# Embedding gate and final norm of a hybrid decoder step on 384 and 192 tokens instead of 288 and 288

## The chip, the cores and the metric

One of the cores of a Trainium2 chip runs the whole program: one inference step of a one-layer decoder for 576 tokens, 512 of a prompt and 64 of samples. The metric is the device time of one execution in microseconds (us). The engines are TensorE (PE, its weight loads shown as PEld), VectorE (DVE), ScalarE (ACT), GpSimd (POOL) and SyncE (SP), whose queue issues the transfers.

## The reference, cut to what matters

The change touches the end of the step: the gate by the per-layer embedding, and the final norm.

```python
gate = jax.nn.sigmoid(rmsnorm(x, lp['ple_norm_g']) @ lp['ple_gate_w'])
x = x + gate * (pe.astype(x.dtype) @ lp['ple_proj'])
...
y_prompt = rmsnorm(y_p, final_norm_g)
y_sample = rmsnorm(y_s, final_norm_g)
```

Here rmsnorm(x, g) is x times the inverse root of the mean square over the 1024 channels, times g. Everything is float32.

## The kernel before, in words

Activations lie transposed: eight tiles x1[0] to x1[7] (named res in the profile) hold 128 channels each on the partitions, with all T = 576 tokens along the row. A matrix product of 1024 by 1024 is therefore 8 output tiles m times 8 input tiles k. To keep float32 accuracy at the faster data type float32r, each weight and each activation is split into a high and a low part (wh, wl; xb0h, xb0l and so on), and each product is three matmuls: high by high, high weight by low activation, low weight by high activation. An output tile of some tokens takes 24 matmuls that add into one bank of PSUM.

The 576 tokens are worked in two halves of HF = 288. For the end of the step:

- `norm_half` makes the ple norm of one half for all eight tiles: DVE scales (L268, xnf), ACT rounds to the high part (L269, xb*k*h), DVE or POOL subtracts for the low part (L270, xb*k*l; POOL for odd k). Both halves are issued ahead of the next step.
- ple_proj is multiplied for all tokens; ACT copies it to the tiles pps (pp, L1383).
- The eight gate weights are loaded and split ahead of use (tiles wg, acth/actl, wh/wl), then the four heads' mLSTM matrices kv are loaded (L1395) into the same ring of nine acth/actl buffers, so that all but the first wait for gate matmuls.
- For each half, for each m: 24 matmuls (`dense_half`, L193); ACT takes tanh of half of it (gth, L1402); DVE multiplies by pps (L1403) and adds into x1[m] (L1404); ACT squares (L253) and DVE adds the square to acc (L254); the last m is squared on DVE (L251).
- Then `rms_half`: three matmuls with acc as weights and a column of ones sum over the channels (L234); DVE scales and adds EPS (L235, rsc); POOL raises to the power -0.5 (L216); ACT spreads the columns (L238, rsb); PE transposes back to rows (L241). DVE multiplies the eight tiles by that and by the gain (yo, L1410), and SP sends them out in five transfers (L1411).
- At the very end the state's matrices, four matmuls a head (L1416), a copy (co, L1418) and a transfer (L1419).

PSUM gives the gates three banks in turn. Tile pools give buffers by tag; a tile that takes a buffer again waits for the last use of it. The tag "u" with two buffers holds gth and co, "y" two, "ac" two, "ws" three. The order on each engine is set by a scheduler from the program and its own estimates; each engine's queue then runs strictly in that order, so what is listed first also waits first.

Of the kernel before, what the change touches and what calls it, by code (L numbers as in the profile page):

```python
# [7 lines left out]
F32 = mybir.dt.float32  # L8
F32R = mybir.dt.float32r
AF = mybir.ActivationFunctionType  # L10
ALU = mybir.AluOpType
# [4 lines left out]
P = 128  # L16
D = 1024
# [4 lines left out]
HF = T // 2  # L22
KD = D // P
NFF = 22
RT = 14
EPS = 1e-6
# [69 lines left out]
def build(tc, nc, I, O):  # L96
    from contextlib import ExitStack

    V, S, G, TE, SY = nc.vector, nc.scalar, nc.gpsimd, nc.tensor, nc.sync
# [9 lines left out]
    with st0:  # L109
# [8 lines left out]
        def bank(tag="m", name="pm"):  # L118
            if tag == "d" and turn:
                tag = turn[0]  # L120
                turn.append(turn.pop(0))
            return ps.tile([P, 512], F32, tag=tag, name=name, bufs=nbufs[tag])
# [5 lines left out]
        def vcol(name, k=0, rows=P):  # L128
            return vec[0:rows, VEC[name] + k:VEC[name] + k + 1]
# [6 lines left out]
        ones = cc("ones")  # L136
# [47 lines left out]
        def dense_half(pm, ws, xs, hf, ks=None):  # L184
            c = slice(hf * HF, (hf + 1) * HF)
            n = len(xs)
            for k in ks or range(n):
                half_k(pm, ws, xs[k], k, n, c)
# [25 lines left out]
        def inv_sqrt(t, n):  # L214

            G.tensor_tensor(t, t, nhalf[0:t.shape[0], :].to_broadcast([t.shape[0], n]), ALU.pow)  # L216
# [10 lines left out]
        HB = (0, P, HF - P)  # L227

        def rms_half(pl, acc, hf, pt="m"):

            pm = bank(pt)
            cols = pl.tile([P, 3], F32, tag="rsc", name="rsc", bufs=2)
            for w, o in enumerate(HB):
                TE.matmul(pm[:, w:w + 1], acc[:, hf * HF + o:hf * HF + o + P], ones[:, 0:1], start=True, stop=True)  # L234
            V.tensor_scalar(cols, pm[:, 0:3], 1.0 / D, EPS, ALU.mult, ALU.add)  # L235
            inv_sqrt(cols, 3)
            bc = pl.tile([P, 3, P], F32, tag="rsb", name="rsb", bufs=2)
            S.copy(bc, cols.unsqueeze(2).to_broadcast([P, 3, P]))  # L238
            b = bank(pt)
            for w, o in enumerate(HB):  # L240
                TE.transpose(b[:, o:o + P], bc[:, w, :], ident)  # L241
            return b[:, 0:HF]

        def add_squares(pl, acc, x, k, hf, eng=None, on_v=False):
            c = slice(hf * HF, (hf + 1) * HF)
            if k == 0:
                (eng or V).tensor_tensor(acc[:, c], x[:, c], x[:, c], ALU.mult)
            else:
                sq = pl.tile([P, HF], F32, tag="sq", name="sq", bufs=3)
                if on_v:  # L250
                    V.tensor_tensor(sq, x[:, c], x[:, c], ALU.mult)  # L251
                else:
                    S.activation(sq, x[:, c], AF.Square)  # L253
                (eng or V).tensor_tensor(acc[:, c], acc[:, c], sq, ALU.add)  # L254
# [121 lines left out]
        with ExitStack() as stn:  # L376
            npool = pool(stn, "n1")
            acc = npool.tile([P, T], F32, name="acc")
# [13 lines left out]
            pm = bank("m")  # L392
# [60 lines left out]
            for hf in range(2):  # L453
                if hf:
                    norm_half(npool, xt, rsr[:, half(1)], 1, "norm1_g", xs1)
                for k in range(KD):
                    for i in range(2):
                        TE.matmul(lps["if"][hf][:, 0:HF], w2[k // 4][:, k % 4, :], xs1[k][i][:, half(hf)],
                                  start=k == 0 and i == 0, stop=k == KD - 1 and i == 1)
# [762 lines left out]
        rpool = pool(stF, "res")  # L1222
        x1 = [rpool.tile([P, T], F32, name=f"res{m}") for m in range(8)]
        acc = rpool.tile([P, T], F32, tag="acc", name="acc")
# [39 lines left out]
        xs2 = new_split(pool(stS, "xn2", side="right"), "xb")  # L1264
# [3 lines left out]
        with ExitStack() as stw:  # L1268
# [5 lines left out]
            for hf in range(2):  # L1274
                c = slice(hf * HF, (hf + 1) * HF)
                for m in range(8):
                    pm = bank("d", "pd")
# [15 lines left out]
        fp = pool(stf_, "ffn")  # L1293
# [63 lines left out]
        for g, (j0, nj) in enumerate(GR):  # L1357
            acts = [up(j0 + j) for j in range(nj)]
            if g == 2:
                SY.dma_start(O["o_fconv"], o_f)  # L1360
                pes = []
                for k in range(2):
                    pt = fp.tile([P, T], F32, tag="ac", name="pe", bufs=2)
                    SY.dma_start(pt, I["pe"][k])
                    pes.append(split(fp, "act", pt, bufs=ACT))
            for m in range(8):
                pss = dense(I["f_down"][m, :, j0:j0 + nj, :], acts)
                for hf in range(2):
                    c = slice(hf * HF, (hf + 1) * HF)
# [14 lines left out]
        wg = []  # L1384
# [7 lines left out]
        for h in range(4):  # L1392
            kv.append([fp.tile([P, 4, n], F32, tag=t, name="kv", bufs=ACT) for t, n in (("acth", P), ("actl", 129))])
            for t, c in zip(kv[h], (slice(0, 512), slice(512, 1028))):
                SY.dma_start(t, d_kv[h][:, c].rearrange("p (w x) -> p w x", w=4))  # L1395
        for hf in range(2):
            c = slice(hf * HF, (hf + 1) * HF)
            for m in range(8):
                pm = bank("d", "pd")
                dense_half(pm, wg[m], xs2, hf)  # L1400
                th = fp.tile([P, HF], F32, tag="u", name="gth", bufs=2)
                S.activation(th, pm[:, 0:HF], AF.Tanh, scale=0.5)  # L1402
                V.scalar_tensor_tensor(th, th, 1.0, pps[m][:, c], ALU.add, ALU.mult)  # L1403
                V.scalar_tensor_tensor(x1[m][:, c], th, 0.5, x1[m][:, c], ALU.mult, ALU.add)  # L1404
                add_squares(rpool, acc, x1[m], m, hf, on_v=m == KD - 1)
            rs = rms_half(rpool, acc, hf, "mr"[hf])
            for k0, n, t, b in ((0, 2, "y", 2), (2, 2, "ac", 2), (4, 2, "y", 2), (6, 1, "ac", 2), (7, 1, "ws", 3)):
                yo = fp.tile([P, n, HF], F32, tag=t, name="yo", bufs=b)
                for k in range(k0, k0 + n):
                    V.scalar_tensor_tensor(yo[:, k - k0, :], x1[k][:, c], vcol("final_norm_g", k), rs, ALU.mult, ALU.mult)  # L1410
                SY.dma_start(O["o_y"][k0:k0 + n, :, c].rearrange("k p t -> p k t"), yo[:, 0:n, :])  # L1411

        for h in range(4):
            pc = bank("scsr"[h])
# [105 lines left out]
```

## Time and profile before

| | us |
|---|---|
| median of three runs | 1073.62 |
| the three runs | 1073.53, 1073.62, 1078.61 |
| the profiled execution | 1070.66 |
| its span | 1068.8 |
| first gate matmul, from the span's start | 1002.58 |
| last gate matmul starts | 1055.31 |
| final scalings of the second half start | 1061.28 |

The profile is one execution with times from the start of its span; the span is 1.86 us shorter than the execution's own time. The granted TensorE clock was 0.996 of full over the span. The chain of waits is read backwards from the last instruction: at each step it names what released the work that ended last. In the timelines a row has start, length, engine, line, operation, output and inputs, and in brackets the idle time before it with what ended that.

### The profile page before, as it was taken

What the parts mean: (1) busy time and instruction counts of PE and PEld (TensorE: products, weight loads), DVE (VectorE), ACT (ScalarE), POOL (GpSimd) and SP (SyncE); (2) the same over time, 40 slices, a digit from 0 to 9 for tenths busy, and PEclk for the clock granted to TensorE, in tenths of its full rate; (3) what the DMA queues carried; (4) which work ended last, traced back from release to release, by engine and by line L of the source; (5) the groups of instructions that cost most, each with busy time, mean ns of one, the idle gap of its engine ahead of it and who ended that gap; (6) DMA issues with size and microseconds to landing.
All of it is one profiled execution on the core that took longest, in us unless ns stands there. A gap on an engine that the chain in (4) does not pass through costs nothing.

```text
span 1068.8 us, 23108 instructions
## 1 busy us (share of the span) xinstructions
PE 1045.1 (98%) x8991; PEld 1009.0 (94%) x8991; DVE 777.0 (73%) x1645; ACT 508.8 (48%) x1072; POOL 254.5 (24%) x394
## 2 busy tenths in 40 slices
PE   8899999999999999999999999999999999999996
PEld 7899999999989988999999999999999999999996
DVE  7887657876786676356775799945998569975864
ACT  7684634462553344334343465522565236553822
POOL 7622112221131021001401253200343005410300
PEclk9999999999999999999999999999999999999999
DMA  7243412442342322446850312322233322342513
GB/s 252 95 127 93 108 53 58 103 141 60 88 143 75 81 84 91 143 151 234 263 181 1 116 37 93 110 90 75 85 99 97 102 70 90 94 117 67 165 40 123
DMA packets 90894, 114.74 MB, mean 107 GB/s; under 512 B 35617, under 2 KB 45217, under 8 KB 90785
## 3 DMA queue, kind: packets, MB, share of 16 engines
q1 hardware_dynamic: 90784, 113.27, 34.7%
q8 instruction: 70, 1.15, 0.4%
q14 instruction: 40, 0.32, 0.1%
HBM read 94.79 MB, written 18.45 MB: 106 GB/s over the span
## 4 chain that ended last, share of the span: by engine, by line
PE 90%; DVE 4%; DMA 4%; ACT 1%; issue 1%; SPq 0%; POOLq 0%; DVEq 0%; ACTq 0%
PE pd L193 55%; PE pd L306 20%; PE pm L655 1%; PE pm L1106 1%; PE pm L1136 1%; PE pm L835 1%; PE pm L809 1%; DMA yin<-d_y 1%; PE pm L910 1%; DVE xnf L268 1%; PE pm L917 1%; PE pm L1199 1%; PE pm L775 0%; DMA d_y<-og 0%; DMA wr<-i_w_out 0%
## 5 line engine op out<-in xcount | busy, mean ns | idle before, releaser
L169 ACT CAST wh<-wr 128x512 fp32r<-128x512 f32 (+2 forms) x170 | 101.7, 599 | 173.4 <-PE pd L193 140.7
L170 DVE TENSOR_TENSOR wl<-wr,wh 128x512 fp32r<-128x512 f32 (+2 forms) x170 | 118.8, 702 | 82.4 <-ACT wh L169 80.8
L193 PE MATMUL pd<-actl,wh 128*128 128x288 f32 x384 | 111.9, 295 | 0.0
L193 PE MATMUL pd<-acth,wl 128*128 128x288 f32 x384 | 111.4, 295 | 0.0
L193 PE MATMUL pd<-acth,wh 128*128 128x288 f32 x384 | 110.3, 295 | 0.0
L193 PEld LDWEIGHTS pd<-actl,wh 128*128 128x128 f32 x384 | 71.8, 188 | 0.0
L193 PEld LDWEIGHTS pd<-acth,wl 128*128 128x128 f32 x384 | 71.6, 188 | 0.0
L193 PEld LDWEIGHTS pd<-acth,wh 128*128 128x128 f32 x384 | 71.1, 188 | 0.1
L294 ACT CAST wh<-ws 128x512 fp32r<-128x512 f32 x76 | 47.1, 619 | 48.9 <-PE pd L306 24.8
L295 DVE TENSOR_TENSOR wl<-ws,wh 128x512 fp32r<-128x512 f32 x76 | 58.1, 765 | 8.4 <-ACT wh L294 7.9
L300 POOL TENSOR_TENSOR ws<-wr 128x512 f32<-128x512 f32 x19 | 31.7, 1670 | 96.9 <-DVE wl L295 54.1
L294 ACT CAST wh<-wr 128x512 fp32r<-128x512 f32 x57 | 35.3, 619 | 38.5 <-PE pd L306 24.0
L1333 POOL COPY o_f<-u 128x2 f32<-128x2 f32 x22 | 26.6, 1209 | 110.8 <-DVE u L1330 109.2
L295 DVE TENSOR_TENSOR wl<-wr,wh 128x512 fp32r<-128x512 f32 x57 | 39.5, 693 | 7.3 <-ACT wh L294 7.2
L216 POOL TENSOR_TENSOR rsc<-rsc,nhalf 128x3 f32<-128x3 f32 x8 | 9.3, 1167 | 131.1 <-DVE rsc L235 131.1
L1342 DVE SCALAR_TENSOR_TENSOR y<-u,vec,y 128x592 f32<-128x592 f32 x44 | 38.5, 875 | 1.2 <-ACT y L1340 1.0
L253 ACT ACTIVATE sq<-res 128x288 f32<-128x288 f32 x40 | 17.7, 445 | 36.0 <-DVE res L1279 18.5
L193 PE MATMUL pd<-mgh,ol 128*128 128x288 f32 x112 | 33.0, 296 | 0.0
L193 PE MATMUL pd<-mgl,oh 128*128 128x288 f32 x112 | 33.0, 295 | 0.0
L193 PE MATMUL pd<-mgh,oh 128*128 128x288 f32 x112 | 32.8, 295 | 0.0
L1370 DVE TENSOR_TENSOR res<-res,pd 128x288 f32<-128x288 f32 x48 | 20.9, 450 | 15.7 <-PE pd L193 15.5
L193 PE MATMUL pd<-xa0h,wh 128*128 128x288 f32 x86 | 26.4, 307 | 3.0 <-ACT zr L352 1.6
(825 smaller groups left out, 3949.4 us busy)
## 6 DMA issues: line engine op xcount, KB each, us to landing
wr<-i_w_in SPq DMA_DIRECT2D x92, 256.0 KB
wr<-i_f_up SPq DMA_DIRECT2D x88, 256.0 KB
wr<-i_f_down SPq DMA_DIRECT2D x32, 256.0 KB
d_th<-gst SPq DMA_DIRECT2D x16, 288.0 KB
th<-d_th SPq DMA_DIRECT2D x16, 288.0 KB
wr<-i_w_br SPq DMA_DIRECT2D x16, 256.0 KB
wr<-i_w_out SPq DMA_DIRECT2D x16, 256.0 KB
wr<-i_ple_gate SPq DMA_DIRECT2D x16, 256.0 KB
```

What stands on the lines that cost most here:

```text
L169: S.copy(wh[:, 0:nk, :], wr[:, 0:nk, :])
L170: V.tensor_tensor(wl[:, 0:nk, :], wr[:, 0:nk, :], wh[:, 0:nk, :], ALU.subtract)
L193: TE.matmul(pm[:, 0:HF], w[:, k % 4, :], a[:, c], start=k == 0 and i == 0, stop=k == n - 1 and i == 2)
L253: S.activation(sq, x[:, c], AF.Square)
L268: V.scalar_tensor_tensor(xn, xt[k][:, c], vcol(gname, k), rs, ALU.mult, ALU.mult)
L294: S.copy(wh, w)
L295: V.tensor_tensor(wl, w, wh, ALU.subtract)
L300: e.tensor_tensor(t, a, b, ALU.add)
L306: TE.matmul(pm[:, 0:HF], w[a][:, k, :], xs[k][b], start=not more and k == 0 and i == 0, stop=k == 3 and i == 2, skip_group_check=more)
L1333: G.tensor_copy(o_f[:, j, 0:2], u[:, TP:TP + 2])
L1342: V.scalar_tensor_tensor(y, u[:, i:i + 592], w(i), y, ALU.mult, ALU.add)
L1370: V.tensor_tensor(x1[m][:, c], x1[m][:, c], pss[hf][:, 0:HF], ALU.add)
```

## The change

The gate and the final norm run on a first group of 384 tokens and a second of 192. The matmuls are written out in the loop (L1409 of the changed program). `rms_half` becomes a call of `rms_part`, which takes several operands for the column sums and any blocks of columns (three of 128 for 384 tokens; two of 128 that overlap for 192). The square of the last tile (sqw) is no longer added into acc, but is a second operand of the column sums. The square of the first tile goes straight from ACT into acc. The first group's outputs are eight single tiles from "y" and "ws"; the second's are three pairs on DVE and one pair, for the first two tiles, that POOL multiplies by a copy of the norm's rows and ACT scales by the gain.

```diff
+        def rms_part(pl, accs, c0, width, blocks, pt):
...
-            for w, o in enumerate(HB):
-                TE.matmul(pm[:, w:w + 1], acc[:, hf * HF + o:hf * HF + o + P], ones[:, 0:1], start=True, stop=True)
+            for w, o in enumerate(blocks):
+                for i, (a, z) in enumerate(zip(accs, (c0, 0))):
+                    TE.matmul(pm[:, w:w + 1], a[:, z + o:z + o + P], ones[:, 0:1], start=i == 0, stop=i == len(accs) - 1)
...
-        for hf in range(2):
-            c = slice(hf * HF, (hf + 1) * HF)
+        for g, (c0, w, blocks) in enumerate(((0, 384, (0, P, 2 * P)), (384, 192, (0, 64)))):
+            c = slice(c0, c0 + w)
             for m in range(8):
-                pm = bank("d", "pd")
-                dense_half(pm, wg[m], xs2, hf)
-                th = fp.tile([P, HF], F32, tag="u", name="gth", bufs=2)
-                S.activation(th, pm[:, 0:HF], AF.Tanh, scale=0.5)
+                pm = bank("d", "pd")[:, 0:w]
+                for k in range(KD):
+                    wh, wl = wg[m][k // 4]
+                    for i, (a, b) in enumerate(((wh, 0), (wh, 1), (wl, 0))):
+                        TE.matmul(pm, a[:, k % 4, :], xs2[k][b][:, c], start=k == 0 and i == 0, stop=k == KD - 1 and i == 2)
+                th = fp.tile([P, 384], F32, tag="u", name="gth", bufs=2)[:, 0:w]
+                S.activation(th, pm, AF.Tanh, scale=0.5)
...
-                add_squares(rpool, acc, x1[m], m, hf, on_v=m == KD - 1)
-            rs = rms_half(rpool, acc, hf, "mr"[hf])
-            for k0, n, t, b in ((0, 2, "y", 2), (2, 2, "ac", 2), (4, 2, "y", 2), (6, 1, "ac", 2), (7, 1, "ws", 3)):
+                if m == 0:
+                    S.activation(acc[:, c], x1[m][:, c], AF.Square)
+                else:
+                    sq = fp.tile([P, 384], F32, tag="ac", name="sqw", bufs=2)[:, 0:w]
+                    if m < KD - 1:
+                        S.activation(sq, x1[m][:, c], AF.Square)
+                        V.tensor_tensor(acc[:, c], acc[:, c], sq, ALU.add)
+                    else:
+                        V.tensor_tensor(sq, x1[m][:, c], x1[m][:, c], ALU.mult)
+            rs = rms_part(rpool, (acc, sq), c0, w, blocks, "mr"[g])
+            n0 = 0
+            if g:
...
+                rsc = fp.tile([P, 192], F32, tag="u", name="rsc2", bufs=2)
+                S.copy(rsc, rs)
+                yo = fp.tile([P, 2, 192], F32, tag="ac", name="yo2", bufs=2)
+                for k in range(2):
+                    G.tensor_tensor(yo[:, k], x1[k][:, c], rsc, ALU.mult)
+                    S.activation(yo[:, k], yo[:, k], AF.Copy, scale=vcol("final_norm_g", k))
+                SY.dma_start(O["o_y"][0:2, :, c].rearrange("k p t -> p k t"), yo)
+                n0 = 2
+            step = 1 + g
+            for i, k0 in enumerate(range(n0, KD, step)):
+                t, nb = ("ws", 3) if i % 2 and not g else ("y", 2)
+                yo = fp.tile([P, step, w], F32, tag=t, name="yo", bufs=nb)
```

On PE, where the gates begin, stood the following before. The outputs pd_13497, pd_13527 and pd_13559 are the gates of tiles m = 0, 1 and 2 in the three banks; xb0h and xb0l are the two parts of the norm's tile k = 0; the last name is the weight.

```order
L193 MATMUL pd_13497<-xb0h_7372,wg_13389 128x288
L193 MATMUL pd_13497<-xb0l_7373,wg_13389 128x288
L193 MATMUL pd_13497<-xb0h_7372,wg_13390 128x288
L193 MATMUL pd_13497<-xb1h_7374,wg_13389 128x288
L193 MATMUL pd_13497<-xb1l_7375,wg_13389 128x288
L193 MATMUL pd_13497<-xb1h_7374,wg_13390 128x288
L193 MATMUL pd_13497<-xb2h_7376,wg_13389 128x288
L193 MATMUL pd_13497<-xb2l_7377,wg_13389 128x288
```

The same place on PE in the changed program:

```order
L1409 MATMUL pd_13497<-xb0h_7372,wg_13389 128x384
L1409 MATMUL pd_13497<-xb0l_7373,wg_13389 128x384
L1409 MATMUL pd_13497<-xb0h_7372,wg_13390 128x384
L1409 MATMUL pd_13527<-xb0h_7372,wg_13399 128x384
L1409 MATMUL pd_13527<-xb0l_7373,wg_13399 128x384
L1409 MATMUL pd_13559<-xb0h_7372,acth_13410 128x384
L1409 MATMUL pd_13559<-xb0l_7373,acth_13410 128x384
L1409 MATMUL pd_13559<-xb0h_7372,actl_13411 128x384
L1409 MATMUL pd_13497<-xb1h_7374,wg_13389 128x384
L1409 MATMUL pd_13559<-xb1h_7374,acth_13410 128x384
L1409 MATMUL pd_13497<-xb1l_7375,wg_13389 128x384
```

Before, the first tile's gate ran through all k at once. Now the first three tiles go abreast, k by k, and each k needs tokens of both halves of the norm.

At PE's end before, behind the last gate matmul (pd_14004), come the state's matmuls of the four heads (kv), the column sums (acc) and the transposes (rsb):

```order
L193 MATMUL pd_14004<-xb7h_7386,actl_13477 128x288
L1416 MATMUL pm_14067<-kv_13482,kv_13481 128x129 x4
L1416 MATMUL pm_14075<-kv_13486,kv_13485 128x129 x4
L1416 MATMUL pm_14083<-kv_13490,kv_13489 128x129 x4
L234 MATMUL pm_14036<-cst_67,acc_6683 128x1 x3
L241 MATMUL pm_14045<-cst_67,rsb_14043 128x128 x3
L1416 MATMUL pm_14091<-kv_13494,kv_13493 128x129 x4
```

PE's end in the changed program, with sqw the last tile's square:

```order
L1409 MATMUL pd_14012<-xb7h_7386,actl_13477 128x192
L1446 MATMUL pm_14084<-kv_13486,kv_13485 128x129 x4
L239 MATMUL pm_14043<-cst_67,acc_6683 128x1
L239 MATMUL pm_14043<-cst_67,sqw_14041 128x1
L239 MATMUL pm_14043<-cst_67,acc_6683 128x1
L239 MATMUL pm_14043<-cst_67,sqw_14041 128x1
L246 MATMUL pm_14053<-cst_67,rsb_14051 128x128 x2
L1446 MATMUL pm_14100<-kv_13494,kv_13493 128x129 x4
L1446 MATMUL pm_14092<-kv_13490,kv_13489 128x129 x4
```

The first head's four matmuls have moved ahead, between the third and the fourth gate tile of the first group; two heads now stand behind the transposes.

At ACT's end before, behind the last tanh (gth), stand three copies of the state, the spreading of the norm and the fourth copy:

```order
L1402 ACTIVATE gth_14029<-pd_14004 128x288
L1418 COPY co_14072<-pm_14067 128x129
L1418 COPY co_14080<-pm_14075 128x129
L1418 COPY co_14088<-pm_14083 128x129
L238 COPY rsb_14043<-rsc_14037 128x384
L1418 COPY co_14096<-pm_14091 128x129
```

And in the changed program, where rsc2 is the copy of the norm's rows and yo2 the pair that POOL has multiplied:

```order
L1411 ACTIVATE gth_14037<-pd_14012 128x192
L243 COPY rsb_14051<-rsc_14044 128x256
L1428 COPY rsc2_14056<-pm_14053 128x192
L1448 COPY co_14081<-pm_14076 128x129
L1432 ACTIVATE yo2_14058<-yo2_14058,vec_66 128x192 x2
L1448 COPY co_14089<-pm_14084 128x129
L1448 COPY co_14097<-pm_14092 128x129
L1448 COPY co_14105<-pm_14100 128x129
```

All four copies of the state now stand behind the transposes, three of them behind the scalings of yo2. Up to the gates the order on every engine is as it was.

More of the change, by code (lines that the diff above doesn't have):

```diff
@@ L229, in rms_half @@
         def rms_half(pl, acc, hf, pt="m"):
+            return rms_part(pl, (acc,), hf * HF, HF, HB, pt)
+        def rms_part(pl, accs, c0, width, blocks, pt):
             pm = bank(pt)
-            cols = pl.tile([P, 3], F32, tag="rsc", name="rsc", bufs=2)
-            for w, o in enumerate(HB):
[L234 to L238, printed above, removed]
+            n = len(blocks)
+            cols = pl.tile([P, 3], F32, tag="rsc", name="rsc", bufs=2)[:, 0:n]
+            for w, o in enumerate(blocks):
+                for i, (a, z) in enumerate(zip(accs, (c0, 0))):
+                    TE.matmul(pm[:, w:w + 1], a[:, z + o:z + o + P], ones[:, 0:1], start=i == 0, stop=i == len(accs) - 1)
+            V.tensor_scalar(cols, pm[:, 0:n], 1.0 / D, EPS, ALU.mult, ALU.add)
+            inv_sqrt(cols, n)
+            bc = pl.tile([P, 3, P], F32, tag="rsb", name="rsb", bufs=2)[:, 0:n]
+            S.copy(bc, cols.unsqueeze(2).to_broadcast([P, n, P]))
             b = bank(pt)
-            for w, o in enumerate(HB):
+            for w, o in enumerate(blocks):
                 TE.transpose(b[:, o:o + P], bc[:, w, :], ident)
-            return b[:, 0:HF]
+            return b[:, 0:width]
         def add_squares(pl, acc, x, k, hf, eng=None, on_v=False):
@@ L1403, in build @@
                 V.scalar_tensor_tensor(th, th, 1.0, pps[m][:, c], ALU.add, ALU.mult)
                 V.scalar_tensor_tensor(x1[m][:, c], th, 0.5, x1[m][:, c], ALU.mult, ALU.add)
-                add_squares(rpool, acc, x1[m], m, hf, on_v=m == KD - 1)
-            rs = rms_half(rpool, acc, hf, "mr"[hf])
-            for k0, n, t, b in ((0, 2, "y", 2), (2, 2, "ac", 2), (4, 2, "y", 2), (6, 1, "ac", 2), (7, 1, "ws", 3)):
[L1408 to L1411, printed above, removed]
+                if m == 0:
[7 more added lines that the diff above has]
+                        V.tensor_tensor(sq, x1[m][:, c], x1[m][:, c], ALU.mult)
@@ L1413, in build @@
+            step = 1 + g
+            for i, k0 in enumerate(range(n0, KD, step)):
+                t, nb = ("ws", 3) if i % 2 and not g else ("y", 2)
+                yo = fp.tile([P, step, w], F32, tag=t, name="yo", bufs=nb)
+                for k in range(step):
+                    V.scalar_tensor_tensor(yo[:, k], x1[k0 + k][:, c], vcol("final_norm_g", k0 + k), rs, ALU.mult, ALU.mult)
+                SY.dma_start(O["o_y"][k0:k0 + step, :, c].rearrange("k p t -> p k t"), yo)
         for h in range(4):
```

## The prediction

> **What bounds the kernel now.** I read the page first, then the chain of waits over the last 110 us, then the timelines of the gate stage engine by engine. The page:
>
> ```profile
> span 1068.8 us, 23108 instructions
> PE 1045.1 (98%) x8991; PEld 1009.0 (94%) x8991; DVE 777.0 (73%) x1645; ACT 508.8 (48%) x1072; POOL 254.5 (24%) x394
> ```
>
> TensorE (PE) is busy nearly all the time. The change lies in the last 66 us. The chain of waits there, as start, length, what (two stretches of gate matmuls left out at the dots):
>
> ```profile
> 1003.41 31.07 PE pd L193 x231
> 1034.47 0.56 PE pm L234 x6
> ...
> 1039.68 0.33 PE pm L241 x3
> 1040.01 15.60 PE pd L193 x117
> 1055.61 2.68 PE pm L1416 x24
> 1058.29 0.63 PE pm L234 x6
> ...
> 1059.22 0.89 POOLq L1516
> ...
> 1060.13 0.52 ACT rsb L238
> ...
> 1060.70 0.56 PE pm L241 x3
> ...
> 1061.28 0.51 DVE yo L1410
> ...
> 1062.22 2.55 DVE yo L1410 x6
> ```
>
> From 1003.41 to 1058.9 PE itself is the chain: gate matmuls (L193), column sums (L234), transposes (L241), the mLSTM state's matmuls (L1416). Only from there on is it a serial tail, through VectorE (DVE), GpSimd (POOL), ScalarE (ACT) and PE, to the final scalings (L1410). The stages view (PE busy, weight loads, DVE, ACT, POOL, clock, DMA) says the same of the first stretch:
>
> ```profile
> 1002.60:1034.50 31.90, 31.60 (x236) 31.37 (x236) 26.18 (x53) 15.74 (x38) 5.49 (x5) 1.00 0.31 92
> ```
>
> PE 31.60 of 31.90 us, at the full granted clock (1.00), while DVE at 26.18 is close behind: it makes the gate's inputs in this very stretch. So whatever lengthens PE's queue here lengthens the run, and only what shortens the 10 us behind 1058.9 can win it back. The predicted sum is made against this execution, 1070.66 us with a span of 1068.8.
>
> **Matmul widths, 288+288 becoming 384+192.** The columns streamed stay the same: 384 matmuls of 288 become 192 of 384 and 192 of 192. The first row above gives 15.60/117 = 0.1333 us from start to start at 288 columns. Two other places in the program show other widths of the same data type; weight loads are PEld:
>
> ```profile
> 122.16 0.39 PE L1094 MATMUL pm<-Mrow,selr 128*128 128x512 f32 x1
> ...
> 122.38 0.29 PE L193 MATMUL pd<-xa2h,wh 128*128 128x288 f32 x1
> ```
>
> ```profile
> 461.77 0.19 PEld L1109 LDWEIGHTS pm<-Mrow,selr 128*128 128x128 f32 x1
> 461.90 0.22 PE L1109 MATMUL pm<-Mrow,selr 128*128 128x128 f32 x1
> 461.90 0.19 PEld L193 LDWEIGHTS pd<-xa0h,wl 128*128 128x128 f32 x1
> 461.96 0.35 PE L193 MATMUL pd<-xa0h,wl 128*128 128x288 f32 x1
> 462.01 0.19 PEld L193 LDWEIGHTS pd<-xa1h,wh 128*128 128x128 f32 x1
> ```
>
> 512 columns take 0.22, so about 0.0004 us per column, and 384 columns 0.1333 + 96 x 0.0004 = 0.173. Downwards the same line would give 0.094 for 192. But the 128-column matmul at 461.90 shows a floor: the next matmul starts after 0.06, yet the weight load behind it starts only 0.11 after the one before (461.90 to 462.01). Each gate matmul brings its own 128x128 weights, so I price 192 columns at 0.11. The six one-column matmuls at 1058.29 (0.63/6 = 0.105) sit at the same floor, with nothing to stream. The bounds are 0.094 (loads cost nothing) and 0.133 (no gain from fewer columns). Sum: 192 x (0.173 - 0.1333) = +7.6, 192 x (0.11 - 0.1333) = -4.5, so **+3.1 us**, with bounds 0.0 and +7.6.
>
> The Trainium skill, page "TensorE: Matmul & The Clock Gate", section "Back-to-back issue gap", gives N/2.4 + 2.5 ns for a warm matmul of N columns, with no weight load in it: 162.5 and 82.5 ns, and by it the stage would not change at all. The rows contradict it at 288 columns already (0.1333 against 122.5 ns).
>
> **The first group reaches into the second half's norm.** Before, the first half's gates need columns 0 to 287 of xb0 to xb7. Now they need 0 to 383, so both halves of the ple norm, and the second is still being made. PE's first gate matmuls now, and the last step of the second half's tiles (h by ACT, l by DVE or POOL):
>
> ```profile
> 1002.58 0.40 PE L193 MATMUL pd<-xb0h,wg 128*128 128x288 f32 x1 [0.61 <-ACT pp L1383]
> 1002.82 0.29 PE L193 MATMUL pd<-xb0l,wg 128*128 128x288 f32 x1
> 1003.41 0.40 PE L193 MATMUL pd<-xb0h,wg 128*128 128x288 f32 x1 [0.30 <-DVE wg L155]
> ```
>
> ```profile
> 1002.75 0.44 ACT L269 CAST xb0h<-xnf 128x288 fp32r<-128x288 f32 x1
> 1004.31 0.64 DVE L270 TENSOR_TENSOR xb0l<-xnf,xb0h 128x288 fp32r<-128x288 f32 x1
> 1005.76 0.82 POOL L270 TENSOR_TENSOR xb1l<-xnf,xb1h 128x288 fp32r<-128x288 f32 x1 [1.13 <-ACT xb1h L269]
> 1008.88 0.45 DVE L270 TENSOR_TENSOR xb2l<-xnf,xb2h 128x288 fp32r<-128x288 f32 x1
> 1015.83 0.45 DVE L270 TENSOR_TENSOR xb6l<-xnf,xb6h 128x288 fp32r<-128x288 f32 x1
> ```
>
> The order of DVE, ACT and POOL up to there is unchanged but for gate operations that move out, so I keep these times. PE's queue is strict: its second gate matmul waits for xb0l at 1004.95. Nine more bring it to 1006.6, where xb1l (1006.58) is just there. Eleven more bring it to 1008.5, and it waits for xb2l until 1009.4. From there 51 of the 72 matmuls of the first three tiles run through (xb6l, at 1016.3 now, comes as it is asked for if the gate operation that has left DVE's queue ahead of it brings 0.7), to 1009.4 + 51 x 0.173 = 1018.2. Without waits the 72 would have had to begin at 1018.2 - 12.5 = 1005.7. Before, two are done by the third's start, 1003.41, so the dense run begins in effect at 1003.1. **+2.6 us**, bounds +1.7 (no wait for xb2l) and +3.3 (xb6l as late as now).
>
> **Other PE work.** Four of the state's matmuls (8 of the 24 records of 2.68 us) move from the tail, where they covered the square and sum, into the gates: **+0.9**. The column sums of the first group take two operands, 12 records for 6 at 0.56: **+0.6**. So the last gate matmul starts 3.1 + 2.6 + 0.9 + 0.6 = 7.2 us later.
>
> **The serial tail.** Its rows, and two 512-column rows for the slope:
>
> ```profile
> 1055.31 0.30 PE L193 MATMUL pd<-xb7h,actl 128*128 128x288 f32 x1
> 1055.64 0.41 ACT L1402 ACTIVATE gth<-pd 128x288 f32<-128x288 f32 x1 [1.27 <-PE pd L193]
> 1056.09 0.46 DVE L1403 SCALAR_TENSOR_TENSOR gth<-gth,pp 128x288 f32<-128x288 f32 x1 [1.22 <-ACT gth L1402]
> 1057.57 0.46 DVE L254 TENSOR_TENSOR acc<-acc,sq 128x288 f32<-128x288 f32 x1
> ```
>
> ```profile
> 1016.57 0.68 DVE L170 TENSOR_TENSOR actl<-wr,acth 128x512 fp32r<-128x512 f32 x1
> 1008.43 0.63 ACT L169 CAST wh<-wr 128x512 fp32r<-128x512 f32 x1
> ```
>
> A column costs DVE (0.68 - 0.46)/224, ACT much the same, so 96 fewer save 0.1 an instruction: tanh, two products and the square -0.4; the addition into acc (0.46 and the step to it) -0.5; rsb on 256 for 384 columns -0.1; two transposes for three -0.1. The column sums behind the square stay at six records. POOL's power, on two columns for three, I take as unchanged. **-1.1 us**, bounds -0.8 and -1.4.
>
> **From the transposes to the end.** Before, DVE's eight scalings run from 1061.28, the last output is issued at 1065.0, and the program ends 7.5 us after 1061.28. The rows on landings, and POOL's slowest subtraction in this stage:
>
> ```profile
> 1056.83 2.48 SPq L1419 DMA_DIRECT2D o_C_p<-co  x3
> 1058.69 0.27 ACT L1418 COPY co<-pm 128x129 f32<-128x129 f32 x1 [0.99 <-DMA o_C_p<-co]
> L1411 SPq DMA_DIRECT2D o_y<-yo x10: 382/406/1069, 1042.0 to 1065.0; - x10
> 1002.94 1.69 POOL L270 TENSOR_TENSOR xb7l<-xnf,xb7h 128x288 fp32r<-128x288 f32 x1 [2.74 <-ACT xb7h L269]
> ```
>
> DVE's part shrinks to six scalings of 2.55/6 - 0.1, about 0.33, but two round trips enter. The third pair of scalings takes the buffer of the first, so it waits for that output's landing: pair ready 0.7, issued 1.15 behind an o_C_p, landing between 1.86 (1056.83 to 1058.69, 64.5 KB) and 3.8 (last issue to the program's end) later, say 2.5, then 0.7, then issue at 4.4. On ACT, the state's copies stand behind the two yo2 scalings, which wait for POOL: copy 0.35, two products at 2/3 of 0.82, a scaling 0.3, so the second co is ready at 2.25, its landing at 4.3 frees the buffer of the fourth, which is issued at 4.7. From a last issue to the end it is 3.8 before, less for a small one, say 3.4: 8.0 against 7.5. **+0.5**, bounds -0.3 and +1.7; the upper one has POOL at 1.69 x 2/3 twice. I take 0.82, since DVE's scalings read one operand from PSUM, and the 1.69 stood beside DVE subtractions of two SBUF tiles.
>
> Sum: 7.2 - 1.1 + 0.5 = **+6.6 us**: a profiled execution of 1077.3, and against the median shown (1073.62, 0.28% above the profiled 1070.66) **1080.2**.
>
> **Rivals.** A measurement of this kernel can tell about 0.5% (5.4 us) from no change.
>
> 1. *Loads hidden, not slower*: if the weight loads hide behind 80 ns of streaming, 192 columns cost 0.094 and the matmul term is 0. Then +3.5, 1077.1. It decides as soon as the spacing falls below about 0.104. For it: the matmul at 461.96 started 0.06 after. Against: the load spacing of 0.11 at that place. This is the skill's rule above. 12%.
> 2. *The front wait hidden*: DVE reaches the second half's tiles earlier because PE and DVE meet differently, and the 2.6 goes. +4.0, 1077.6. Against: DVE, ACT and POOL keep their order and DVE has no gap there. 9%.
> 3. *A new wait in the second group*: the first group's scalings have two "y" and three "ws" buffers for eight outputs, so DVE waits for outputs that stand in SP's queue behind the state loads, which wait for PE:
>
> ```profile
> SPq L1395 <- PE pd L193: 27.4, 3, 25.4
> ```
>
> The last of these loads is let go when the fourth tile of the second group is half done. Behind the waiting scaling in DVE's queue stand the second group's products, and behind those ACT's next tanh and PE's banks. I put DVE's wait at 2 us with over 5 us of gates still to come, enough to catch up. With landings 2 us later it isn't, and PE or the tail loses 1.5 to 3: 1081.7 to 1083.2. 10%.
> 4. *192 columns as dear as 288*: +11.1, 1084.7, 4%.
>
> Left: 4% for faster by more than 0.5%, for which I see no mechanism (rivals 1 and 2 together still give +0.9).
>
> **The numbers.** My forecast has 61%, on its own 1078.6 to 1082.0; about 8 of it lie under 1079.0. Slower by over 0.5%: 53 + 10 + 4 = 0.67; within: 8 + 12 + 9 = 0.29; faster 0.04. The range 1077.0 to 1083.0 takes in rivals 1 and 2 and most of 3.
>
> **What would show it.** Right: 192-column gates spaced at 0.11; PE idle about 1.6 us before the second gate matmul and 0.9 before an xb2l one; last gate matmul about 7 us later; the transposes 4.8 us behind it; the last issue an o_C_p. Wrong: spacing under 0.104, no PE gap on xb0l, or the end less than 7 us behind the transposes.

## The result and the profile after

The changed kernel takes 1083.47 us (median of 10 runs, 1081.82 to 1088.01), the kernel before 1074.19 (10 runs, 1071.36 to 1081.18). The ratio is 1.0083, interval 1.0064 to 1.0102: slower, by 6.9 to 11 us. The forecast was slower by 6.6; 1083.47 lies 0.5 us above the range.

The page of the changed kernel's profiled execution (1086.85 us):

```profile
span 1084.7 us, 23126 instructions
PE 1057.0 (97%) x8998; PEld 1017.6 (94%) x8998; DVE 775.2 (71%) x1639; ACT 510.9 (47%) x1077; POOL 255.0 (24%) x396
```

Its span is 15.9 us longer, where the medians of the runs differ by 9.3. Part of that has nothing to do with the change. Up to the gates both kernels issue the same instructions in the same order; a good mark there is the ple norm's first scaling of its first half on DVE, in the kernel before and in the changed one:

```profile
994.38 1.79 DVE L268 SCALAR_TENSOR_TENSOR xnf<-res,vec,pm 128x288 f32<-128x288 f32 x4 [0.29 <-PE pm L241]
```

```profile
1001.43 1.79 DVE L273 SCALAR_TENSOR_TENSOR xnf<-res,vec,pm 128x288 f32<-128x288 f32 x4 [0.29 <-PE pm L246]
```

7.05 us are lost ahead of it. The changed kernel's second trace, further down, loses 2.8 there, so this is the execution and not the change; about 3.9 of the 7.05 come where the first trace has two stretches of half clock, at 313.99 and 395.91, that the trace of before has not. From this mark to the end it is 74.4 us before and 83.3 after: **+8.9**, which is what the ratio of the runs says too. So all comparisons of traces below count from this mark. (The expectations call it the second half's first scaling; it is the first half's.) Three points divide the rest, in us behind the mark:

| | before | after | difference | forecast |
|---|---|---|---|---|
| 72nd gate matmul starts | 18.33 | 25.27 | +6.94 | +5.5 (72 x 0.0397 + 2.6) |
| last gate matmul starts | 60.93 | 70.50 | +9.57 | +7.2 |
| last group's first scaling on DVE | 66.90 | 75.80 | +8.90 | +6.1 |
| end | 74.4 | 83.3 | +8.9 | +6.6 |

Every step but the last goes the way that was forecast. What is missing lies ahead of the last gate matmul, most of it in the first 72. PE there (start, length, tiles; the first rows of the group and some later ones):

```profile
1010.98 0.44 PE L1409 MATMUL pd<-xb0h,wg 128*128 128x384 f32 x1 [1.27 <-ACT xb0h L274]
1012.05 0.44 PE L1409 MATMUL pd<-xb0l,wg 128*128 128x384 f32 x1 [0.63 <-DVE xb0l L275]
...
1014.77 0.69 PE L1409 MATMUL pd<-xb1l,wg 128*128 128x384 f32 x1
1015.26 0.52 PE L1409 MATMUL pd<-xb1h,wg 128*128 128x384 f32 x1
1015.58 0.52 PE L1409 MATMUL pd<-xb2h,wg 128*128 128x384 f32 x1
...
1018.04 0.34 PE L1409 MATMUL pd<-xb2h,wg 128*128 128x384 f32 x1
...
1021.58 0.34 PE L1409 MATMUL pd<-xb5l,wg 128*128 128x384 f32 x1
```

The second gate matmul waits for xb0l: 10.62 us behind the mark, where the forecast had 1004.95 - 994.38 = 10.57. But behind that matmuls of 384 columns stand 0.32 us apart (1015.26 to 1015.58), and only from 1017 on 0.177 (20 steps from 1018.04 to 1021.58). The stages view names the reason (PE, weight loads, DVE, ACT and POOL busy, granted clock, DMA share, GB/s):

```profile
1010.31:1013.72 3.41, 1.99 (x8) 1.42 (x9) 3.41 (x8) 3.41 (x9) 1.23 (x2) 1.00 0.67 221
1013.72:1017.13 3.41, 3.29 (x11) 2.77 (x10) 3.41 (x5) 2.81 (x8) 2.32 (x2) 0.50 0.69 189
1017.13:1020.54 3.41, 3.41 (x21) 3.41 (x21) 3.41 (x8) 2.82 (x6) 1.02 (x1) 1.00 0.75 239
```

Behind 3.41 us in which PE was busy for 1.99, the granted clock halves for 3.41 us. These cuts are not free to choose. The half-clock stretches of this trace start at 313.99, 395.91, 1013.72 and 1075.16, which are 24, 181 and 18 times 3.413 us apart, and the cuts here and below lie on that grid of each trace. In the kernel before PE was busy for 2.74 us of the stretch around its own small waits, and the clock stayed:

```profile
1002.21:1005.62 3.41, 2.74 (x18) 2.51 (x19) 3.41 (x8) 3.41 (x11) 1.69 (x1) 1.00 0.63 191
```

The clock is not all that is new in this stretch. xb1l, ready 12.20 us behind the mark before, is ready at 13.29 here, because ACT came to it 0.7 later, behind a longer wait for a weight load, and POOL's own step took 1.23 for 0.82 (ACT in the kernel before, then in the changed one):

```profile
999.94 0.62 ACT L169 CAST acth<-wr 128x512 fp32r<-128x512 f32 x1 [0.45 <-DMA wr<-i_ple_gate]
```

```profile
1007.68 0.62 ACT L169 CAST acth<-wr 128x512 fp32r<-128x512 f32 x1 [1.15 <-DMA wr<-i_ple_gate]
```

The chain from there on, stretches left out at the dots:

```profile
1027.04 0.89 PE pm L1446 x8
...
1053.91 1.03 PE pm L239 x10
...
1059.27 12.95 PE pd L1409 x116
1072.23 0.34 ACT gth L1411
...
1073.38 0.37 DVE sqw L1422
...
1073.80 0.84 PE pm L239 x6
...
1074.97 0.70 POOL rsc L216
1075.70 0.41 ACT rsb L243
...
1076.15 0.70 PE pm L246 x2
1076.88 0.33 ACT rsc L1428
1077.23 1.40 DVE yo L1440 x4
```

The state's four matmuls among the gates cost 0.89, 192 columns take 12.95/116 = 0.112, and the tail from last gate matmul to scalings is 5.3 us for 5.97. One step in it is new to the forecast: DVE starts its scalings not behind the transposes (1076.85) but behind ACT's copy rsc2 (1077.21), which reads the same bank of PSUM.

The waits that the forecast and rival 3 spoke of are all there (DVE, ACT, and SP's last issue):

```profile
1063.94 1.14 DVE L1440 SCALAR_TENSOR_TENSOR yo<-res,vec,pm 128x384 f32<-128x384 f32 x2 [2.19 <-DMA o_y<-yo]
...
1080.13 0.74 DVE L1440 SCALAR_TENSOR_TENSOR yo<-res,vec,pm 128x192 f32<-128x192 f32 x2 [1.51 <-DMA o_y<-yo]
```

```profile
1081.81 0.27 ACT L1448 COPY co<-pm 128x129 f32<-128x129 f32 x1 [1.18 <-DMA o_C_p<-co]
```

```profile
1082.11 0.33 SPq L1449 DMA_DIRECT2D o_C_p<-co  x1
```

The first, 2.19 us in the second group, is rival 3's. DVE has caught up by 1068, and PE runs through (116 matmuls in one piece above): it costs nothing.

### The profile page after: what moved, and what is told of

It is laid out like the page before. It is cut to its first block, busy times and chain, and to the rows that moved or that the text cites. A ratio compares the mean times of both kernels' runs of the same rounds, so it can differ in the third digit from the quotient of the medians.

```text
span 1084.7 us, 23126 instructions
## 1 busy us (share of the span) xinstructions
PE 1057.0 (97%) x8998; PEld 1017.6 (94%) x8998; DVE 775.2 (71%) x1639; ACT 510.9 (47%) x1077; POOL 255.0 (24%) x396
## 4 chain that ended last, share of the span: by engine, by line
PE 44%; DVE 5%; DMA 3%; ACT 1%; issue 1%; POOL 0%; SPq 0%; DVEq 0%; ACTq 0%; POOLq 0%
PE pd L193 19%; PE pd L311 19%; PE pd L1409 5%; DMA wr<-i_f_up 1%; DVE wl L170 1%; DMA wr<-i_w_out 0%; DMA d_y<-og 0%; DMA th<-d_th 0%; DVE y L1347 0%; DVE xnf L273 0%; PE pm L239 0%; DMA wr<-i_ple_gate 0%; DMA yin<-d_y 0%; DVE ws L305 0%; DVE ya L1246 0%
## 5 line engine op out<-in xcount | busy, mean ns | idle before, releaser
L170 DVE TENSOR_TENSOR wl<-wr,wh 128x512 fp32r<-128x512 f32 (+2 forms) x170 | 118.8, 703 | 83.1 <-ACT wh L169 80.8
L216 POOL TENSOR_TENSOR rsc<-rsc,nhalf 128x3 f32<-128x3 f32 (+1 forms) x8 | 9.2, 1148 | 140.6 <-DVE rsc L240 140.6
L1375 DVE TENSOR_TENSOR res<-res,pd 128x288 f32<-128x288 f32 x48 | 20.9, 450 | 15.7 <-PE pd L193 15.5
L1200 POOL TENSOR_TENSOR VS<-VS,cst 128x258 fp32r<-128x258 f32 x16 | 10.4, 657 | 77.5 <-ACT VS L1190 39.1
```

Of the source, the lines that this page charges most:

```text
L170: V.tensor_tensor(wl[:, 0:nk, :], wr[:, 0:nk, :], wh[:, 0:nk, :], ALU.subtract)
L1200: G.tensor_tensor(m.rearrange("p (b x) -> p b x", b=2), v.unsqueeze(1).to_broadcast([P, 2, 129]), cc("bmask", 8)[:, b0:b0 + 2].unsqueeze(2 ...
L1375: V.tensor_tensor(x1[m][:, c], x1[m][:, c], pss[hf][:, 0:HF], ALU.add)
```

## The experiments

Their marks, as differences from the kernel before in us, and the ratio of the times with its interval:

| run | last gate matmul | first last scaling | end | time |
|---|---|---|---|---|
| changed kernel | +9.57 | +8.90 | +8.9 | 1.0083 (1.0064 to 1.0102) |
| changed kernel again | +8.64 | +7.72 | +8.7 | 1.0080 (1.0053 to 1.0107) |
| 288 and 288 | +0.66 | +1.04 | +2.5 | 1.0022 (1.0004 to 1.0041) |
| 192, then 384 | +5.18 | +6.43 | +9.8 | 1.0113 (1.0078 to 1.0149) |
| 320, then 256 | +6.50 | +5.90 | +7.3 | 1.0075 (1.0046 to 1.0104) |
| 256, then 320 | +1.04 | +1.95 | +5.6 | 1.0046 (1.0031 to 1.0062) |
| fillers at the front | +8.40 | +7.73 | +7.8 | 1.0073 (1.0052 to 1.0094) |
| split alone | +9.43 | +8.57 | +7.9 | 1.0072 (1.0055 to 1.0089) |
| sums alone | +0.66 | +1.27 | +1.2 | 1.0010 (0.9990 to 1.0030) |
| scalings alone | -0.32 | +0.12 | +1.5 | 1.0018 (0.9997 to 1.0038) |
| own buffers at the end | +8.88 | +8.14 | +6.8 | 1.0088 (1.0063 to 1.0114) |
| fillers and own buffers | +9.20 | +8.46 | +7.0 | 1.0048 (1.0033 to 1.0062) |
| products ahead, 288 and 288 | -0.32 | +0.04 | +1.1 | 1.0008 (0.9994 to 1.0022) |

The intervals are 3 to 8 us wide, so the steps of 1 or 2 us between runs are told by the marks of one trace each, not by the times. How far such marks spread for one kernel is known from a single pair: the changed kernel's two traces differ by 0.9, 1.2 and 0.2 us. The kernel before has one trace.

**The split against the rest.** The changed kernel with two groups of 288:

```diff
-for g, (c0, w, blocks) in enumerate(((0, 384, (0, P, 2 * P)), (384, 192, (0, 64)))):
+for g, (c0, w, blocks) in enumerate(((0, 288, (0, P, 160)), (288, 288, (0, P, 160)))):
...
```

> The changed kernel with two groups of 288 tokens in place of 384 and 192; all its other edits stay (last squares straight into the column sums, two last scalings on GpSimd and ScalarE, single-tile outputs of the first group). Theory A (the uneven split itself costs: 4.2 us by the widths, since in the changed kernel's trace 384 columns are spaced at 0.177 us and 192 at 0.112 against 0.133 at 288, and 3 to 4 us by the first group's wait for the second half's norm): both go, and what is left is the column sums' second operand (0.6), state matmuls that move into the gates (up to 0.9) and the end, so 0 to +2.5 us against the kernel before. Theory B (the other edits cost most of the loss: the new round trips of buffers at the end, the state matmuls at half clock): +4 us or more.

PE's front is as in the kernel before, without a wait on the norm:

```profile
1006.35 0.40 PE L1409 MATMUL pd<-xb0h,wg 128*128 128x288 f32 x1 [0.61 <-ACT pp L1388]
1006.59 0.29 PE L1409 MATMUL pd<-xb0l,wg 128*128 128x288 f32 x1
```

+2.5 us, theory A's upper end; 6.4 of the 8.9 us went with the uneven split. Of the 2.5, 0.7 lie in the column sums, 0.4 in the tail and 1.4 behind the first scaling.

**Width or wait.** The short group first, so that it lies in the first half's norm:

```diff
+for g, (c0, w, blocks) in enumerate(((0, 192, (0, 64)), (192, 384, (0, P, 2 * P)))):
...
-            step = 1 + g
+            step = 1
...
```

> The changed kernel with the short group first: tokens 0 to 191, then 192 to 575. The 192 columns of the first group lie in the first half's norm, so PE's wait for xb0l, xb1l and xb2l of the second half goes, and the widths stay as they are. The last group is 384 wide, so its last scalings go out as single tiles, and its serial tail is some 0.5 to 1 us longer than with 288. Theory A: the widths' 4.2 us stay, the front's 3 to 4 go: +5 to +7.5 us against the kernel before, and the spacing is again 0.112 and 0.177. Theory C (the front's wait is nearly all of it, and the widths cost under 1 us): +1 to +3.

Up to the last gate matmul it went as theory A says: spacings 0.112 and 0.177, granted clock 1.00 at the front, +5.18, of which 4.2 is the widths. The forecast of the whole failed, since the end behind the first scaling took 10.9 us for 7.5. The two runs at 320 and 256, in both orders, differ in where the wait lies and not in the widths:

```diff
+for g, (c0, w, blocks) in enumerate(((0, 320, (0, P, 192)), (320, 256, (0, P)))):
...
```

> The changed kernel with groups of 320 and 256 tokens. The first group still reaches into the second half's norm, by 32 columns. By the slope from 288 to 384 (0.00046 us a column) 320 columns take 0.148 us and 256 take 0.119, so the widths' cost is 0 if 256 columns still lie above the floor that 192 show. Theory A: the widths' 4.2 us go and the front's wait stays, with a low granted clock (0.5) for some 3 us behind it as in the changed kernel: +3.5 to +6.5 us. Theory D (the widths and the floor are nearly all, the wait is caught up later): 0 to +2.

```diff
+for g, (c0, w, blocks) in enumerate(((0, 256, (0, P)), (256, 320, (0, P, 192)))):
...
-            step = 1 + g
+            step = 1
...
```

> The changed kernel with groups of 256 and 320 tokens, in that order: the same two widths as the run with 320 first, but the first group's columns lie in the first half's norm. Theory A: no wait at the front, granted clock 1.00 there, widths for nothing: 0 to +2.5 us against the kernel before, so 3 to 4 us less than with 320 first. Theory D: no difference to the run with 320 first.

320 columns are spaced at 0.147 us in both traces and 256 at 0.119 and 0.120: together 0.266, as twice 0.133, so the widths cost nothing here. With 320 first the last gate matmul comes 5.46 us later than with 256 first. At the 72nd it is 6.35, and 2.0 of these are only the wider columns coming first; the other 4.4 us are the wait with its clock. The rest, 1.1, is other PE work, such as column sums of three blocks for two in the first group (1.13 for 0.68). The stages view with 320 first, up to and behind 1010.21; the second gate matmul starts at 1010.01:

```profile
1006.80:1010.21 3.41, 1.01 (x5) 0.55 (x5) 3.41 (x8) 3.41 (x10) 1.48 (x1) 1.00 0.51 127
1010.21:1013.62 3.41, 3.41 (x14) 3.41 (x14) 3.41 (x6) 3.41 (x10) 1.73 (x2) 0.50 0.59 190
```

Theory D falls. The time with 320 first, +8 us, lies above the range that I gave, as does that of 256 first with +5. With 256 first the surplus is at the end: in both runs whose last group is wide I let each tile go out alone. The fourth state copy on ACT, with 256 first:

```profile
1074.06 0.27 ACT L1448 COPY co<-pm 128x129 f32<-128x129 f32 x1 [4.76 <-DMA o_C_p<-co]
```

It waits 4.76 us for a buffer whose transfer stands in SP's queue behind three outputs. That is the price of my edit, not of the order.

**The clock.** PE kept busy where it waits, with products that nobody reads:

```diff
+pz = bank("s")
+for n, e in ((8, 256), (5, 384)):
+    for _ in range(n):
+        TE.matmul(pz[:, 0:e], wg[0][0][0][:, 0, :], xs2[0][0][:, 0:e], start=True, stop=True)
 for g, (c0, w, blocks) in enumerate(((0, 384, ...
```

> The changed kernel with 13 more matmuls on PE at the front of the gates, 8 of 256 columns on xb0h's first half and 5 of 384, into a PSUM bank that nobody reads: useless work that lies where PE waits for xb0h and xb0l. Theory A: the low granted clock (0.50) behind the front's wait comes from PE's idleness there; with the fillers it stays at 1.00, and the last gate matmul comes about 1.3 us earlier than in the changed kernel (69.2 us behind VectorE's first scaling of the second half's norm, where the changed kernel has 70.5 and the kernel before 60.9). Against the kernel before +6.5 to +8.5 us. Theory E (the clock falls for another reason, or the waits for xb1l and xb2l set the pace anyway): 70.3 or later, +8.5 us or more.

The second gate matmul is where it was (10.62 behind the mark), the clock stays, and the wait for xb2l is now in the open, as forecast:

```profile
1007.88:1011.29 3.41, 2.90 (x18) 2.38 (x17) 3.41 (x8) 3.41 (x10) 1.50 (x1) 1.00 0.60 177
1011.29:1014.71 3.42, 3.33 (x18) 2.73 (x16) 3.42 (x6) 3.24 (x8) 1.73 (x2) 1.00 0.62 182
```

```profile
1015.15 0.44 PE L1413 MATMUL pd<-xb2l,wg 128*128 128x384 f32 x1 [0.53 <-DVE xb2l L275]
```

The last gate matmul starts at 69.33, where theory A had 69.2: more work on PE, and 1.17 us earlier. The times cannot tell 1.2 us, so theory E is refuted by the trace alone. Not all of the 1.17 is the clock: here ACT's weight load was not late, and xb1l was ready at 12.37. By an estimate, the changed kernel's eleven matmuls from xb1l (13.34) on would at full clock have reached xb2l at 15.29 and waited for it until 15.45, against 15.16 here, so 0.3 is the late xb1l and xb2l (15.41 for 15.11) and about 0.9 the clock. The changed kernel once more, as it is:

> The changed kernel once more, as it is, for a second trace of it. Theory A: the time up to the second half's norm scalings differs from the first trace's 1001.4 us (it is the same instructions as before the change, where it was 994.4), but from there to the end it is 83.3 us again within 0.5, with the granted clock at 0.50 for about 3 us behind the front's wait: +8 to +9.5 us. Theory E (the low clock at the front was a chance of that one execution): no 0.50 there, and 82.2 us or less.

```profile
1003.80:1007.21 3.41, 1.43 (x8) 0.94 (x7) 3.41 (x8) 3.41 (x9) 1.45 (x1) 1.00 0.44 126
1007.21:1010.62 3.41, 2.85 (x9) 2.86 (x10) 3.41 (x7) 3.41 (x10) 1.34 (x3) 0.50 0.72 221
```

Low again, and the end 83.1 behind the mark. But the low stretch began earlier, partly while PE still waited for xb0l (at 1007.77). It ended 13.5 behind the mark, ahead of xb2l (14.95), for which PE would have had to wait anyway; in the first trace it lasted until 15.7. Its last gate matmul is only 0.24 later than with fillers. So the clock's price differs between executions of one kernel, by where the grid falls: about 0.9 and 0.24 us in these two.

**Parts alone.** The split alone, with squares, scalings and last outputs as in the kernel before:

```diff
+                    V.tensor_tensor(acc[:, c], acc[:, c], sq, ALU.add)
-            rs = rms_part(rpool, (acc, sq), c0, w, blocks, "mr"[g])
+            rs = rms_part(rpool, (acc,), c0, w, blocks, "mr"[g])
...
```

> The groups of 384 and 192 tokens alone: the last squares are added into the column sum as in the kernel before, and all eight last scalings run on VectorE in the buffers of the kernel before. Theory A: the last gate matmul 9.0 us later than before (widths 4.2, front 3.9, moved state matmuls 0.9), the tail and the end some 0.5 to 1 us shorter for 96 columns fewer: +7.5 to +9 us against the kernel before, so as much as the whole change. Theory B (the other edits add their 2.4 us of the 288 and 288 run on top): +6 to +7 us.

+7.9 in the trace, +7.7 (5.9 to 9.6) by the times, where theory A stands; but here the low clock lasted twice as long:

```profile
1009.93:1013.34 3.41, 2.72 (x8) 2.72 (x9) 3.41 (x7) 3.41 (x9) 1.18 (x3) 0.50 0.79 226
1013.34:1016.76 3.42, 3.42 (x12) 3.42 (x12) 3.42 (x7) 1.83 (x4) 0.87 (x1) 0.50 0.74 201
```

The 72nd gate matmul comes 1.71 us later than with fillers (25.81 against 24.10), where the changed kernel's two traces had 1.17 and 0.24. With those prices the +7.9 would be 7.3 or 6.4, an estimate, against +8.9 and +8.7 for the whole change: the split is most of the loss, and the other edits add some 1.6 to 2.3 us, nearer to theory B. The stretch behind the last gate matmul, which the front's clock does not touch, says the same: 11.9 us to the end here, 12.8 in the whole change. One trace of the split alone does not settle it, and the times cannot.

The two other edits, each alone on groups of 288. First the sums, whose diff touches the last tile's addition (against the kernel before's way of summing):

```diff
-                    V.tensor_tensor(acc[:, c], acc[:, c], sq, ALU.add)
-            rs = rms_part(rpool, (acc,), c0, w, blocks, "mr"[g])
+            rs = rms_part(rpool, (acc, sq), c0, w, blocks, "mr"[g])
```

> The kernel before with one edit: the last tile's squares go straight into the column sums, in both groups of 288; scalings and outputs as before. Theory A: +0.6 us for six more records in the first group's column sums, -0.5 for the addition that leaves the tail: -0.5 to +1 us, no difference that can be measured. Theory F (the sums carry the 2.4 us of the 288 and 288 run, since state matmuls no longer cover the square): +1.5 us or more.

No difference that can be measured. In the trace the tail is 0.6 us longer, not shorter: the new order puts state matmuls between the sums of acc and those of the square, and the sums of two operands are ten records behind it:

```profile
1066.35 0.12 PE pm L239 x2
1066.47 1.00 PE pm L1433 x8
1067.47 1.02 PE pm L239 x10
```

For the scalings alone the diff is the change's own for them, with w = 288.

> The kernel before with the other edit alone: groups of 288, the squares added as before, two of the last group's scalings on GpSimd and ScalarE, the other six in pairs in two buffers, single tiles in the first group. Theory A: VectorE waits for ScalarE's copy rsc2 (0.4 us) and the buffers' round trips lengthen the end by 1.4 us: +1 to +2.5 us against the kernel before. Theory F: under +0.5 us.

+1.5 in the trace, in theory A's range; by the times it cannot be told from nothing. Both waits are there (DVE):

```profile
1063.31 1.79 DVE L1440 SCALAR_TENSOR_TENSOR yo<-res,vec,pm 128x288 f32<-128x288 f32 x4 [2.61 <-ACT rsc L1428]
1066.59 0.94 DVE L1440 SCALAR_TENSOR_TENSOR yo<-res,vec,pm 128x288 f32<-128x288 f32 x2 [1.50 <-DMA o_y<-yo]
```

**The end.** The changed kernel without the buffers' round trips:

```diff
-t, nb = ("ws", 3) if i % 2 and not g else ("y", 2)
+t, nb = ("ws", 3) if i % 2 or g else ("y", 2)
...
-co = fp.tile([P, 129], F32, tag="u", name="co", bufs=2)
+co = fp.tile([P, 129], F32, tag="xn1", name="co", bufs=4)
```

> The changed kernel without the two round trips at the end: the last group's three pairs of scalings have three buffers (ws), the state's copies four of their own (xn1). Theory A: the end behind the first scaling shortens from 7.5 to some 6.3 us, since the third pair no longer waits for the first pair's landing nor the fourth copy for the second's: 0.8 to 1.5 us less than the changed kernel, +7 to +8.3 us against the kernel before. Rival H (the state matmuls at half clock behind the transposes set the end by themselves): less than 0.4 us gained.

The six scalings run in one piece, and from the first of them to the end it is 6.1 us for 7.5:

```profile
1069.94 2.04 DVE L1440 SCALAR_TENSOR_TENSOR yo<-res,vec,pm 128x192 f32<-128x192 f32 x6 [2.15 <-ACT rsc L1428]
```

Rival H falls by the trace. The times (four runs from 1077.87 to 1085.52) show no gain at all; 2 us are below what they tell. Then both mends at once:

> The changed kernel with both mends at once: the 13 useless matmuls where PE waits at the front, and buffers of their own for the last pairs and the state's copies. Theory A (the terms add up): 1.2 us from the front's clock and some 2 us from the end come off the changed kernel's 83.3 us from the second half's first norm scaling to the end, so 79.8 to 80.6, where the kernel before has 74.4. What is left is the widths' 4.2 us and some 1.5 us of waits on PE: +4.5 to +7 us against the kernel before. Rival H (one mend only moves the wait to the other's place): +7.5 us or more.

The time, +5.2 (3.5 to 6.7), is where theory A has it; the marks are not: +7.0 for 5.4 to 6.2, short of rival H's +7.5. The clock stayed at 1.00, but PE came to xb6h 0.45 us after the matmul before it, for 0.177 otherwise, and lost some more behind it, because ACT had xb6h queued behind a rounding that waited for a weight load (PE, then ACT):

```profile
1017.29 0.62 PE L1413 MATMUL pd<-xb6h,wg 128*128 128x384 f32 x2
```

```profile
1016.28 0.62 ACT L169 CAST wh<-wr 128x512 fp32r<-128x512 f32 x1 [2.24 <-DMA wr<-i_ple_gate]
1016.81 0.43 ACT L274 CAST xb6h<-xnf 128x288 fp32r<-128x288 f32 x1
```

In the run with fillers alone the same rounding started 0.9 us earlier behind the mark (19.53 for 20.44), so the late load looks like chance; one trace of each does not show that the second mend has no part in it.

**A version that beats both?** The kernel before with products prepared ahead; the last group's rms_part makes a second set of transposes, rs2, in a bank of its own:

```diff
+                for k in range(2):
+                    S.activation(xg[:, k], x1[k][:, c], AF.Copy, scale=vcol("final_norm_g", k))
             rs = rms_part(rpool, (acc,), c0, w, blocks, "mr"[g], two=bool(g))
+                S.copy(rsc, rs2)
+                for k in range(2):
+                    G.tensor_tensor(xg[:, k], xg[:, k], rsc, ALU.mult)
```

> The kernel before with its two groups of 288 and its squares as they were, and the idea of the scalings on GpSimd and ScalarE in another form: ScalarE multiplies x1's first two tiles by the norm's weights during the gates, a second set of three transposes puts the scale into a bank of its own, ScalarE copies it from there, and GpSimd multiplies; the state's copies get four buffers of their own. VectorE then has six scalings for eight and waits for nobody. Theory A: nothing changes up to the transposes, and the end behind them is 0.5 to 1 us shorter than the 7.5 us of the kernel before: -1 to +0.3 us, below what a measurement can tell, but to be seen in the trace. Rival G (the last landing sets the end whatever VectorE does, or GpSimd's two products take longer than the six scalings): the end stays at 7.4 us or more.

Rival G: DVE's last scaling ends 0.8 us earlier, and the end still takes 8.5 us. SP issues in order, and the second output of scalings stands behind a state transfer, whose matmuls ran at half clock behind the transposes (PE, then SP; in the kernel before's trace these eight records took 1.06 us):

```profile
1066.46 1.93 PE L1443 MATMUL pm<-kv 128*128 128x129 f32 x8
```

```profile
1068.72 0.33 SPq L1446 DMA_DIRECT2D o_C_p<-co  x1
1069.14 0.39 SPq L1438 DMA_DIRECT2D o_y<-yo  x1
```

No version that I tried beats the kernel before.

## Why the prediction was right or wrong

Sign and mechanisms were right: what lengthens PE's queue here lengthens the run. The step that failed is the price of the columns beyond 288, and beside it a clock that was taken as full. The sum was too small by 2.3 us against the traces, and the two terms in which these stand make that up. (Of the 3.3 us between 1080.2 and 1083.47, another 0.6 is the kernel before's own median, 1074.19 over ten runs for 1073.62 over three.)

- **The widths, +3.1, measured +4.2**: 192 x (0.177 - 0.1333) - 192 x (0.1333 - 0.1116) = 8.4 - 4.2. The step that failed is "512 columns take 0.22, so about 0.0004 us per column": 288 at 0.1333 and 384 at 0.177 give 0.00045. One row with a 512-column matmul was too coarse a slope to multiply by 192: the trace has four such places, and the other three, behind other neighbours, read 0.33 to 0.34. The floor was right (0.112 for 0.11), and so were the bounds. Rival 1 asked for less than 0.104 and falls, and with it, for these matmuls, the rule of the Trainium skill that the forecast set beside it.
- **The front's wait, +2.6**: right as the wait that it named. With fillers the 72nd gate matmul starts 24.10 - 18.33 = 5.77 us later, less 72 x 0.0437 for the widths = 2.6. What the step left out is the granted clock: it took the matmuls behind the wait at full speed. The half clock, about 0.9, and the late weight load, 0.3, added 1.2 us in the first trace (70.50 against 69.33 with fillers). I had read 1.00 in the kernel before and carried it over to a place where I had just put in two idle stretches. The Trainium skill, "TensorE: Matmul & The Clock Gate", section "What's actually happening", says that PE's clock is halved by an idle window of about 3.4 us and given back after as long a busy one. By that rule the forecast should have had a rival of up to +1.7 us, an estimate, half of 3.4. The traces agree with the half and with 3.4 us of it (once 6.83), but PE had no idle stretch over 1.3 us here; being busy for 1.99 of 3.41 was enough.
- **Other PE work, +0.9 and +0.6**: measured 0.89 for the state's four matmuls, and 0.14 + 1.03 for the column sums' 0.56.
- **The tail, -1.1, measured -0.67**: from last gate matmul to the square's column sums it became 1.1 shorter (2.98 to 1.88), the norm's steps 0.3. Given back are 0.35 for DVE's wait on ACT's copy, 0.2 for column sums at 0.14 a record instead of 0.105, and 0.15 for two transposes at half clock. The wait belongs to a rule that I had not used: the Trainium skill, "PSUM — Partial Sum Buffer", section "PSUM bank collisions raise a hardware error", tells of a dependency that the compiler's scheduler adds between accesses of two engines to one bank, reads included; DVE's start at 1077.23 behind the copy's end fits it.
- **To the end, +0.5, measured 0.0** (by its own terms, 4.7 + 3.4 against 7.5, the forecast would be +0.6): both round trips are there, the last issue (an o_C_p, as forecast) 4.9 behind the first scaling for 4.7. The landing behind it took 2.6 us for my 3.4. The second trace has 8.5 us for this stretch instead of 7.5, so the bounds hold it.

Together, in the first trace: 6.6 + 1.1 (widths) + 1.2 (clock and late load) + 0.4 (tail) - 0.5 (end) = 8.8 for 8.9. Rival 2 falls, rival 4 too; rival 3's wait happened, and the slack behind it took it in. The range was a little too narrow above, since it gave no room to a clock that the trace of before did not show.

## What to carry to other kernels

Equal tiles are cheap where width has a floor: a pair of widths costs nothing as long as both lie on the straight part (256 and 320 did, 192 and 384 did not). A tile edge that crosses the boundary of how its input is made buys a wait, and a wait that leaves PE half idle for 3.4 us can be paid twice, the second time in clock (0.2 to 1.7 us here, by the execution). For each engine that a change adds to the end, look at what it shares: a bank, a ring of buffers, a queue that issues in order.

## What the runs showed of the hardware

- Spacing of float32r matmuls with their own 128x128 weights: 0.112 us at 192 columns, 0.119 at 256, 0.133 at 288, 0.147 at 320, 0.177 at 384. Straight from 256 to 384, 0.00045 us a column; 192 lie on a floor, since the line would give 0.090.
- At the front of the gates, on each trace's grid of 3.413 us, the granted clock halved behind stretches in which PE was busy for 0.89, 1.01, 1.43, 1.68 and 1.99 us, and stayed behind those with 2.27 and more. It came back after 3.41 us, once after 6.83. The first group reached into the second half's norm without fillers in just these five traces; with fillers, in two traces, the clock stayed.
- That is no limit for all matmuls: behind 1.73 busy us the clock stayed in the sums' trace (515.35 to 518.76), and it halved behind a stretch with PE busy throughout in the changed kernel's (310.57 to 313.99, most of it matmuls of 32 by 32 and of two columns). What decides there is open.
- The same instructions up to the mark took 994.4 to 1002.7 us in the traces of this study: more than the whole effect of the change. Without a mark behind which the kernels differ, two profiled executions cannot be compared at this size.
